# Where the last two projection tiles of a block stand: inside a hand-ordered head, beside sums of squares moved between engines

## The chip, the core and the metric

The kernel runs on one core of a Trainium2 chip. The core has five engines that run their own queues in order and wait for each other through semaphores: TensorE (PE, matmuls; PEld are its weight loads), VectorE (DVE), ScalarE (ACT), GpSimd (POOL) and SyncE (SP, which issues most of the transfers). Matmul results land in PSUM banks; everything else lies in SBUF. The metric is the device time of one execution in microseconds; lower is better. The times are medians of several runs.

## What is computed

A two-layer encoder over two sequences, 256 and 512 tokens, which the kernel keeps side by side as 768 columns. Layer 0 mixes with an mLSTM, layer 1 with windowed attention; each is followed by a gated residual, a modulated norm and a convolutional feed-forward block (FFN):

```python
for l in range(DEPTH):
    mod = jax.nn.silu(c) @ adaln_w[l] + adaln_b[l]
    sh1, sc1, g1, sh2, sc2, g2 = [t[:, None, :] for t in jnp.split(mod, 6, axis=-1)]
    h = rmsnorm(x, norm_g[l, 0]) * (1 + sc1) + sh1
    ...
    y = mlstm_mixer(...) if l % N_MIXERS == 0 else swa_mixer(...)   # both end in "@ w_out"
    x = x + g1 * y
    h = rmsnorm(x, norm_g[l, 1]) * (1 + sc2) + sh2
    x = x + g2 * conv_ffn(h, ffn_w_up[l], ffn_conv_w[l], ffn_conv_b[l], ffn_w_down[l])
return rmsnorm(x, final_g)
```

`rmsnorm` multiplies by `rsqrt(mean(x * x) + EPS)` over the 1024 features. The change touches, in each layer, the end of `@ w_out`, the norm behind it, and the start of `h @ ffn_w_up`.

## The kernel before

**Layout and precision.** Features lie on the 128 partitions, in KC = 8 chunks; tokens run along the free axis. A matrix product in full precision is made of three faster ones: an operand is split into a high part (a rounded copy, made by ScalarE) and a low part (the remainder, a subtraction on VectorE), and high-high, high-low and low-high products are added up in one PSUM bank. `split` (L275) makes `whi` and `wlo` of a weight tile of 128x1024; there are three buffers of each and five of `raw`, into which SP loads.

**The output projection** (`out_proj`, L592) makes 16 tiles: 8 output chunks for the first half of the columns (0 to 383), then 8 for the second half (384 to 767) in the order 5, 6, 7, 4, 0, 1, 2, 3. Below, tile i is the i-th of the 16, from 0. A tile is 24 matmuls of 384 columns (`product`, L632) into one of four fixed banks: tile i takes bank (i + 2) mod 4. Then VectorE adds the gated result to x (`resid`, L590), and ScalarE squares the new x (`Norm.square`, L111). `out_proj` is a generator: the caller runs it as far as its `yield`, then does something else.

**The norm** (`Norm`, L90) has to add up eight squares over chunks and partitions. VectorE adds the squares of the first KC - on_pe chunks into one array (L115; on_pe is 2); TensorE sums the array and the two squares left over the partitions, with a 128x2 constant as the moving operand: 3 arrays x 3 blocks of 128 tokens = 9 matmuls (L146, in the trace `pa<-inv,nt`). ScalarE adds EPS (L150), GpSimd raises to the power -0.5 (L153), and TensorE spreads the result over the partitions (L158, `pa<-kct,nr`). `stages` is a generator whose steps the caller places. `apply` in `combined` (L1095) then scales, shifts and splits the normed values: for the first half at once, for the second half step by step, into combinations called T1, T2, T4, B22 and T3; for T3 it needs the difference of two shifts, `dsh` (L1107).

**The FFN's first product** uses one level of a fast matrix product: B11 and B21 are quarters of the normed values of the first half of the columns, T1 to T4 and B22 belong to the second. `quarters` (L1162) is 12 matmuls of 384 columns for one of them; if `low` is given, it is called after 8 of them. `outset` (L1184) does B11, copies the bank to SBUF (L1189), then adds B21 into the same bank. Sums of weights (`sums`, L1279) are needed as well.

**Who decides the order.** A scheduler orders each engine's instructions by priority and a simulated clock, except in a `manual_schedule` block: there TensorE, ScalarE and VectorE keep the order in which the code is written. `head` (L1257) is such a block; `ffn` runs it for the first pair of hidden tiles, once a layer. Before it, tiles 0 to 14 have been made outside; tile 15 is the first matmul work inside, after two "marks" (L1276, L1277: one matmul each that writes banks 2 and 3, so that later copies into them can be added to). Then come the first quarter, the norm's mean, the second quarter, the spread, and so on; `step()` runs the next part of the norm's generator. `issue_after` (L1420) makes the instructions of the next pair of tiles (`pair`, L1194, whose weight sums run on GpSimd at L1202, L1205, L1206) queue behind named instructions on the same engine.

Of the kernel before, what the change touches and what calls it, by code (L numbers as in the profile page):

```python
# [16 lines left out]
P = 128  # L17
# [67 lines left out]
def pieces(c0, c1):  # L85

    return [(max(c0, s0), min(c1, s1), q) for q, (s0, s1) in enumerate(SEQS) if max(c0, s0) < min(c1, s1)]


class Norm:  # L90
# [16 lines left out]
    def square(self, c):  # L107

        net = self.net
        sq = net.tmp([P, self.n])  # L110
        net.nc.scalar.activation(sq, self.x(c), AF.Square)  # L111
        self.sums.append(sq)
        if 2 <= len(self.sums) and self.count < KC - self.on_pe:
            acc = self.sums[0]
            self.adds.tensor_tensor(acc, acc, self.sums.pop(), ALU.add)  # L115
        self.count += 1

    count = 0

    def begin(self, n):  # L120

        if self.pm is None:
            self.pm = self.net.pa()
            self.sides = [self.pm[:, 2 * b : 2 * b + 2] for b in range(self.n // P)]
            self.done = 0
        for i in range(self.done, n):
            for b, o in enumerate(self.sides):

                self.net.nc.tensor.matmul(
                    o, self.sums[i][:, b * P : (b + 1) * P], self.net.inv,  # L130
                    start=i == b == 0, stop=i == KC - 1, skip_group_check=True,
                )
        self.done = max(self.done, n)

    def stages(self):
# [15 lines left out]
        else:  # L151
            nc.vector.tensor_scalar(r, mean, EPS, None, ALU.add)
        nc.gpsimd.tensor_tensor(r, r, net.mhalf[:, :nb], ALU.pow)  # L153
        yield 2.0
# [13 lines left out]
class Net:  # L168
# [120 lines left out]
    def step(self, gen, n=1):  # L289
        for _ in range(n):  # L290
            next(gen, None)
# [300 lines left out]
    def out_proj(self, u0, act, xt, l, apply):  # L592
# [15 lines left out]

        norms = [Norm(self, xt, half, apply, last=True, adds=self.nc.vector) for half in HALVES]

        self.turn = 1
        todo = tiles()
        if not self.begun:
            first = [next(todo) for _ in range(2)]
            todo = chain(first, todo)
            for i, (z, c, w) in enumerate(first):
                self.product(self.bank[2 + i][:, :H], w, act, 0, H, range(KC - 1))
                self.begun[i] = KC - 1
        for i, (z, c, w) in enumerate(todo):
            if i in (KC, 2 * KC - 1):  # L620
                yield
            c0, c1, _ = HALVES[z]
            o = self.ps()[:, : c1 - c0]
            self.product(o, w, act, c0, c1, range(self.begun.pop(i, 0), KC))
            self.tick(4.2)
            for p0, p1, q in pieces(c0, c1):
                self.resid(xt, o[:, p0 - c0 : p1 - c0], l, 16, c, (p0, p1, q))
            norms[z].square(c)
            if i % KC == KC - 1:
                self.start(HALVES[z], norms[z].stages())  # L630
# [443 lines left out]
    def combined(self, l, i, pool):  # L1074
# [10 lines left out]
        def modulate(b, c, x, pr, rng):  # L1085
            c0, c1, _ = rng
            for p0, p1, q in pieces(c0, c1):
# [5 lines left out]
                nc.scalar.activation(b[:, s], b[:, s], AF.Identity, bias=sh)  # L1093

        def apply(x, pr, rng):  # L1095
            if rng[0] == 0:
                for c in range(KC):
                    full[c] = one(F32)
                    modulate(full[c], c, x, pr, rng)
                    put((self.B11, self.B21)[c // 4], c % 4, full[c])  # L1100
                return
# [4 lines left out]
            sh = lambda c: self.mod[l][:, 24 * i + c, q : q + 1]  # L1106
            dsh = pool.tile([P, 4], F32, name="dsh")  # L1107
            nc.vector.tensor_tensor(
                dsh, self.mod[l][:, 24 * i + 4 : 24 * i + 8, q], self.mod[l][:, 24 * i : 24 * i + 4, q], ALU.subtract
            )  # L1110

# [71 lines left out]

    def outset(self, o, w, r1):  # L1184


        part = lambda i: [t[:, 512 * i : 512 * (i + 1)] for t in w]
        self.quarters(o, part(0), self.B11, True)
        self.nc.scalar.copy(r1[:, col(H) :], o)  # L1189
        yield  # L1190
        self.quarters(o, part(1), self.B21, False)
        self.evict(r1, o)
# [64 lines left out]
    def head(self, u0, last_tile, pool, urows, mark, early):  # L1257
# [21 lines left out]
        def sums(i):  # L1279
            tt = nc.vector.tensor_tensor  # L1280
            s2, s4, s1_, a22 = q[i]
            tt(s1_, s1_, a22, ALU.add)
            nc.scalar.copy(s1[i][0], s1_)
            tt(s2, s1_, s2, ALU.subtract)
            tt(s4, s4, s2, ALU.subtract)
            tt(s1[i][1], s1_, s1[i][0].bitcast(F32), ALU.subtract)
            tt(s1_, a22, s2, ALU.subtract)

        def split(src, to=None):

            hi, lo = to or (self.stg.tile([P, 1024], R, tag=t, name=self.nm(t), bufs=3) for t in ("whi", "wlo"))
            nc.scalar.copy(hi, src)
            return (hi, lo), lambda: nc.vector.tensor_tensor(lo, src, hi.bitcast(F32), ALU.subtract)
# [3 lines left out]
        wa[0] = self.split(ra[0])  # L1297
        sums(0)
        wc[0] = self.split(ra[0])
        for _ in last_tile:  # L1300
            pass
        norm = self.take(HALVES[1])
        step = lambda n=1: [next(norm, None) for _ in range(n)]
        first = self.outset(fixed(0), wa[0], rows[0][0])
        next(first)
        step()
        sums(1)
        wc[1] = self.split(ra[1])
        next(first, None)

        step()
        pa = lambda: self.pa()[:, :H]
# [55 lines left out]
        self.evict(r4, d2)  # L1368
        return act.ins, dve.ins

# [297 lines left out]
```

## Time and profile before

| | |
|---|---|
| median of 3 runs | 1845.19 us (1843.85 to 1846.6) |
| the profiled execution | 1843.78 us |
| its span, first to last instruction | 1842.0 us |
| granted TensorE clock, mean | 0.994 |
| share of the span on the chain that ended last | PE 86%, DVE 6%, DMA 3%, ACT 2%, issue 1%, POOL 1% |

The profile records each instruction of one execution: engine, source line, operation, output and inputs by their names in the program, start and duration. In a timeline row the first two numbers are start and duration in us, `x18` means that 18 instructions were merged into the row, and a bracket gives how long the engine had been idle and what ended it. A row of waits reads "engine, line, waited for engine, line: us in total, times, longest". Matmuls are pipelined, so that their durations overlap; a matmul of 128x384 is followed by the next 0.17 us later. An fp32 matmul of the norm appears as two records. `ps` and `pa` are PSUM banks, `nt` the arrays of squares, `nr` the norm, `slab` large activations. The line is often that of a helper: L254 is any matmul issued through `mm`, L260 and L261 are the two halves of a split.

### The profile page before, as it was taken

The numbers are of one execution on the slowest core, as the hardware profiler recorded it, in microseconds if no ns is written. First come the engines' busy times: TensorE is split into PE (matmuls) and PEld (weight loads), VectorE is DVE, ScalarE is ACT, GpSimd is POOL, SyncE is SP. The second block draws the span as 40 slices with busy tenths as digits, with TensorE's granted clock in tenths as the row PEclk, the third lists the DMA queues.
The fourth block names the chain that finished last, engine by engine and source line by source line (L and its number), as shares of the span: only waits on it lengthen the run. The fifth ranks groups of instructions, "written<-read, shape, count | busy, mean of one in ns | idle before, by whom it ended". The sixth has DMA issues, their size and how long they took to land.

```text
span 1842.0 us, 28931 instructions
## 1 busy us (share of the span) xinstructions
PE 1793.2 (97%) x11290; PEld 1657.4 (90%) x11290; DVE 1367.0 (74%) x2101; ACT 895.3 (49%) x1815; POOL 488.0 (26%) x386
## 2 busy tenths in 40 slices
PE   6999999999999999999999999999999999999997
PEld 3987887889998999999999999889989999999997
DVE  4755676886689877777777757766898777777776
ACT  4443443354456444444444556765564444444443
POOL 1001001021024333333331313430144333333322
PEclk9999999999999999999999999999999999999999
DMA  8344566546312221222223321124122222222212
GB/s 330 119 145 134 172 195 221 164 138 219 101 46 74 76 61 66 69 69 69 69 69 93 104 83 50 53 94 129 50 86 69 69 69 69 69 69 70 69 35 69
DMA packets 64245, 184.48 MB, mean 100 GB/s; under 512 B 6167, under 2 KB 23831, under 8 KB 64108
## 3 DMA queue, kind: packets, MB, share of 16 engines
q1 hardware_dynamic: 64108, 182.63, 30.8%
q8 instruction: 89, 1.46, 0.3%
q14 instruction: 48, 0.39, 0.1%
HBM read 176.17 MB, written 6.43 MB: 99 GB/s over the span
## 4 chain that ended last, share of the span: by engine, by line
PE 86%; DVE 6%; DMA 3%; ACT 2%; issue 1%; POOL 1%; SPq 0%; POOLq 0%; ACTq 0%; DVEq 0%
PE ps L254 27%; PE pa L254 25%; PE ps L1169 10%; PE ps L1172 10%; PE ps L1170 10%; PE pa L1008 1%; DMA slab<-in_adaln_w_dram 1%; DMA raw<-in_w_dram 1%; DVE wlo L261 1%; DVE ada L506 1%; DVE slab L590 1%; DMA raw<-in_adaln_w_dram 0%; PE pa L1172 0%; PE pa L1169 0%; PE pa L1170 0%
## 5 line engine op out<-in xcount | busy, mean ns | idle before, releaser
L260 ACT CAST whi<-raw 128x1024 fp32r<-128x1024 f32 x237 | 247.9, 1048 | 350.4 <-PE pa L254 161.4
L261 DVE TENSOR_TENSOR wlo<-raw,whi 128x1024 fp32r<-128x1024 f32 x237 | 316.6, 1337 | 119.8 <-ACT whi L260 117.3
L254 PE MATMUL pa<-slab,whi 128*128 128x256 f32 (+1 forms) x1472 | 346.6, 331 | 3.2 <-DVE slab L590 3.2
L254 PEld LDWEIGHTS pa<-slab,whi 128*128 128x128 f32 x1472 | 252.7, 188 | 27.5 <-DVE slab L590 4.5
L590 DVE SCALAR_TENSOR_TENSOR slab<-pa,mod,slab 128x256 f32<-128x256 f32 (+1 forms) x368 | 211.2, 592 | 70.8 <-PE pa L254 70.5
L254 PE MATMUL pa<-slab,wlo 128*128 128x256 f32 (+1 forms) x736 | 233.9, 330 | 0.0
L254 PE MATMUL ps<-zh,whi 128*128 128x256 f32 (+1 forms) x560 | 189.0, 339 | 2.3 <-ACT whi L260 1.7
L254 PE MATMUL ps<-zh,wlo 128*128 128x256 f32 (+1 forms) x560 | 184.1, 330 | 2.0 <-DVE wlo L261 2.0
L254 PE MATMUL ps<-zl,whi 128*128 128x256 f32 (+1 forms) x560 | 185.1, 332 | 0.0
L1169 PE MATMUL ps<-zh,whi 128*128 128x384 f32 x504 | 172.3, 342 | 3.6 <-ACT nt L1240 1.8
L1170 PE MATMUL ps<-zl,whi 128*128 128x384 f32 x504 | 169.9, 337 | 0.8 <-DVE zl L1126 0.8
L1172 PE MATMUL ps<-zh,wlo 128*128 128x384 f32 x504 | 168.9, 335 | 0.0
L254 PEld LDWEIGHTS pa<-slab,wlo 128*128 128x128 f32 x736 | 138.5, 188 | 13.1 <-DVE wlo L261 0.4
L1205 POOL TENSOR_TENSOR raw<-raw,raw 128x512 f32<-128x512 f32 x40 | 52.2, 1305 | 330.8 <-DVE wlo L261 259.4
L254 PE MATMUL ps<-slab,whi 128*128 128x384 f32 x512 | 132.0, 339 | 0.9 <-DVE slab L261 0.5
L1402 POOL TENSOR_TENSOR slab<-slab 128x772 f32<-128x772 f32 x44 | 86.5, 1967 | 164.6 <-DVE slab L1390 152.7
L1389 DVE SCALAR_TENSOR_TENSOR slab<-slab,cstt,slab 128x771 f32<-128x771 f32 x88 | 103.6, 1179 | 26.6 <-ACT slab L1387 26.5
L254 PEld LDWEIGHTS ps<-zh,whi 128*128 128x128 f32 x560 | 107.4, 192 | 15.9 <-issue 4.4
L506 DVE SCALAR_TENSOR_TENSOR ada<-raw,silc,ada 128x1024 f32<-128x1024 f32 x84 | 110.6, 1354 | 14.9 <-DMA raw<-in_adaln_w_dram 14.8
L1202 POOL TENSOR_TENSOR raw<-raw 128x512 f32<-128x512 f32 x40 | 68.5, 1712 | 200.1 <-DMA raw<-in_w_dram 169.7
L254 PEld LDWEIGHTS ps<-zh,wlo 128*128 128x128 f32 x560 | 107.2, 192 | 12.2 <-DVE wlo L261 2.9
L254 PEld LDWEIGHTS ps<-zl,whi 128*128 128x128 f32 x560 | 107.4, 192 | 11.9 <-issue 3.4
(291 smaller groups left out, 4265.7 us busy)
## 6 DMA issues: line engine op xcount, KB each, us to landing
raw<-in_w_dram SPq DMA_DIRECT2D x208, 512.0 KB, 3.7
raw<-in_adaln_w_dram SPq DMA_DIRECT2D x84, 512.0 KB, 4.6
slab<-in_x_dram SPq DMA_DIRECT2D x12, 512.0 KB, 6.8
slab<-in_adaln_w_dram SPq DMA_DIRECT2D x12, 512.0 KB, 10.3
slab<-mrows SPq DMA_DIRECT2D x8, 384.0 KB, 5.3
xs<-slab SPq DMA_DIRECT2D x6, 512.0 KB, 3.6
bt<-brow SPq DMA_DIRECT2D x16, 192.0 KB, 3.0
slab<-xs SPq DMA_DIRECT2D x6, 512.0 KB, 6.9
```

What stands on the lines that cost most here:

```text
L254: self.nc.tensor.matmul(out, lhsT, rhs, start=start, stop=stop)
L260: nc.scalar.copy(hi, src)
L261: return nc.vector.tensor_tensor(lo, src, hi.bitcast(F32), ALU.subtract)
L506: stt(acc[:, s], row, w, acc[:, s], ALU.mult, ALU.add)
L590: self.nc.vector.scalar_tensor_tensor(x, o, self.mod[l][:, gc + c, q : q + 1], x, ALU.mult, ALU.add)
L1169: mm(o, wh[:, k], hi[k], start=start and k == 0, stop=False, skip_group_check=True)
L1170: mm(o, wh[:, k], lo[k], start=False, stop=False, skip_group_check=True)
L1172: mm(o, wl[:, k], hi[k], start=False, stop=k == 3, skip_group_check=True)
L1202: tt(q[2], q[2], q[3], ALU.add)
L1205: tt(q[0], q[2], q[0], ALU.subtract)
L1389: stt(y[:, 1:], u[:, :-1], w(0), y[:, 1:], ALU.mult, ALU.add)
L1402: nc.gpsimd.tensor_tensor(y, y, yrow[:, j], ALU.mult)
```

## The change

Half 0 of the norm gets `on_pe` 0 and half 1 gets 1 (`i` of the enumeration): VectorE adds all eight squares of half 0, and seven of half 1. The mean of half 1 is split: `begin(1)` sums the array of seven in the head, ahead of the first quarter, and the last square follows as part of the norm's first step.

`out_proj` yields before tile 14 in place of tile 15, so that tile 14, too, is made inside the head; the weights of tile 15 are drawn (loaded and split) before that yield. Tiles 14 and 15 yield after their product and after their residual and square; their square is added when the head calls `norm.add()`.

In the head, the weight sums of the second pair of tiles and the split behind them go ahead of the first quarter, between the steps of tiles 14 and 15. The norm's first two steps are handed to `outset` as `low`, so they run inside the first and the second quarter. The power's instruction is returned as a third entry of `behind`; as the pair with index 0 takes `behind[0:]` and the one with index 1 `behind[2:]`, GpSimd's work of both next pairs queues behind it. `dsh` is computed at the start of half 0's `apply`.

```diff
@@ Norm
         self.sums.append(sq)
-        if 2 <= len(self.sums) and self.count < KC - self.on_pe:
+        self.count += 1
+        if not self.held:
+            self.add()
+
+    def add(self):
+        if 2 <= len(self.sums) and self.count <= KC - self.on_pe:
             acc = self.sums[0]
             self.adds.tensor_tensor(acc, acc, self.sums.pop(), ALU.add)
-        self.count += 1
+
+    held = False
@@ Norm.begin
-        for i in range(self.done, n):
+        last = min(KC, self.on_pe + 1) - 1
+        for i in range(self.done, min(n, last + 1)):
             for b, o in enumerate(self.sides):
...
-                    start=i == b == 0, stop=i == KC - 1, skip_group_check=True,
+                    start=i == b == 0, stop=i == last, skip_group_check=True,
@@ Norm.stages
-        nc.gpsimd.tensor_tensor(r, r, net.mhalf[:, :nb], ALU.pow)
+        self.power = nc.gpsimd.tensor_tensor(r, r, net.mhalf[:, :nb], ALU.pow)
@@ out_proj
-        norms = [Norm(self, xt, half, apply, last=True, adds=self.nc.vector) for half in HALVES]
+        norms = [Norm(self, xt, half, apply, i, last=True, adds=self.nc.vector) for i, half in enumerate(HALVES)]
+        self.norm = norms[1]
...
-        for i, (z, c, w) in enumerate(todo):
-            if i in (KC, 2 * KC - 1):
+        soon = []
+        for i in range(2 * KC):
+            z, c, w = soon.pop() if soon else next(todo)
+            late = i >= 2 * KC - 2
+            if i == 2 * KC - 2:
+                soon.append(next(todo))
+            if i in (KC, 2 * KC - 2):
                 yield
...
             self.tick(4.2)
+            if late:
+                norms[z].held = True
+                yield
             for p0, p1, q in pieces(c0, c1):
                 self.resid(xt, o[:, p0 - c0 : p1 - c0], l, 16, c, (p0, p1, q))
             norms[z].square(c)
+            if late:
+                yield
@@ combined
+        dsh = pool.tile([P, 4], F32, name="dsh")
+
         def apply(x, pr, rng):
             if rng[0] == 0:
+                s = self.mod[l][:, 24 * i : 24 * i + 8, 0]
+                nc.vector.tensor_tensor(dsh, s[:, 4:], s[:, :4], ALU.subtract)
                 for c in range(KC):
...
-            dsh = pool.tile([P, 4], F32, name="dsh")
-            nc.vector.tensor_tensor(
-                dsh, self.mod[l][:, 24 * i + 4 : 24 * i + 8, q], self.mod[l][:, 24 * i : 24 * i + 4, q], ALU.subtract
-            )
@@ outset
-    def outset(self, o, w, r1):
+    def outset(self, o, w, r1, low=None):
...
-        self.quarters(o, part(0), self.B11, True)
+        self.quarters(o, part(0), self.B11, True, low)
         self.nc.scalar.copy(r1[:, col(H) :], o)
         yield
-        self.quarters(o, part(1), self.B21, False)
+        self.quarters(o, part(1), self.B21, False, low)
@@ head, sums
             tt(s2, s1_, s2, ALU.subtract)
+            yield
             tt(s4, s4, s2, ALU.subtract)
+            yield
             tt(s1[i][1], s1_, s1[i][0].bitcast(F32), ALU.subtract)
             tt(s1_, a22, s2, ALU.subtract)
+            yield
@@ head
         wa[0] = self.split(ra[0])
-        sums(0)
-        wc[0] = self.split(ra[0])
+        ops = [sums(i) for i in range(2)]
+        next(ops[0])
+        next(ops[0])
+        wc[0], low = split(ra[0])
+        next(last_tile)
+        next(last_tile)
+        next(ops[0])
+        low()
+        self.norm.add()
+        next(last_tile)
+        self.norm.begin(1)
+        next(ops[1])
+        next(last_tile)
+        next(ops[1])
+        wc[1], low = split(ra[1])
+        next(ops[1])
+        low()
         for _ in last_tile:
             pass
         norm = self.take(HALVES[1])
         step = lambda n=1: [next(norm, None) for _ in range(n)]
-        first = self.outset(fixed(0), wa[0], rows[0][0])
+        first = self.outset(fixed(0), wa[0], rows[0][0], step)
         next(first)
-        step()
-        sums(1)
-        wc[1] = self.split(ra[1])
         next(first, None)
 
-        step()
...
-        return act.ins, dve.ins
+        return act.ins, dve.ins, self.norm.power.ins
```

## The prediction

> **What bounds the kernel now.** I read the page first, then TensorE's waits over the whole span, then the order of time on each engine around the two heads (layer 0 near 500 us, layer 1 near 1290 us), since the change touches nothing else.
>
> ```profile
> span 1842.0 us, 28931 instructions
> PE 1793.2 (97%) x11290; PEld 1657.4 (90%) x11290; DVE 1367.0 (74%) x2101; ACT 895.3 (49%) x1815; POOL 488.0 (26%) x386
> ```
>
> TensorE (PE) is the bound. An edit pays only if it takes instructions or idle time from PE, and costs only if it puts some in. From the table of PE's waits:
>
> ```profile
> PE ps L1172 <- DVE s1l L261: 2.7, 2, 1.4
> PE pa L254 <- POOL nr L153: 2.5, 4, 1.0
> ...
> PE ps L1169 <- ACT ps L1218: 1.4, 2, 0.7
> ```
>
> Columns: total us, times, longest. Of these only the L153 waits (the power that ends the norm) lie in the stretch that is rewritten. PE there, in order of time (start, duration; a chained matmul starts 0.17 us after the last one, so durations overlap):
>
> ```profile
> 477.63 2.06 PE L254 MATMUL pa<-inv,nt 128*128 128x2 f32 x18
> ...
> 501.36 0.52 PE L254 MATMUL ps<-slab,whi 128*128 128x384 f32 x2
> ...
> 505.57 0.52 PE L254 MATMUL ps<-yh 128*128 128x384 f32 x2
> ...
> 510.12 0.34 PE L1169 MATMUL ps<-yh,whi 128*128 128x384 f32 x1
> ...
> 512.03 0.34 PE L1172 MATMUL ps<-yh,wlo 128*128 128x384 f32 x1
> 512.21 2.06 PE L254 MATMUL pa<-inv,nt 128*128 128x2 f32 x18
> 514.13 0.42 PE L1169 MATMUL ps<-yh,whi 128*128 128x384 f32 x1
> 514.39 0.34 PE L1170 MATMUL ps<-yl,whi 128*128 128x384 f32 x1
> ...
> 516.93 0.93 PE L254 MATMUL pa<-kct,nr 128*128 128x128 f32 x6 [0.47 <-POOL nr L153]
> 517.62 0.42 PE L1169 MATMUL pa<-yh,zh 128*128 128x384 f32 x1
> ```
>
> Half 0's mean stands at 477.63. Tile 14's product starts at 501.36, the two marks at 505.57 with tile 15's product right behind (2 x 0.174 us later, 505.93), the first quarter at 510.12, half 1's mean at 512.21, the second quarter at 514.13; then PE idles 0.47 us for the power before it spreads the norm over the partitions. In layer 1 the same wait is 0.76 us:
>
> ```profile
> 1307.70 0.93 PE L254 MATMUL pa<-kct,nr 128*128 128x128 f32 x6 [0.76 <-POOL nr L153]
> ```
>
> **The change part by part**, per layer, worked in layer 0.
>
> **Squares.** Half 0 now sums all eight squares on VectorE, so its mean takes 3 matmuls in place of 9. The 9 are 18 records; the block is (514.13 - 512.21) / 18 = 0.107 us a record. Twelve records go: **-1.28 us**. Half 1 keeps two sums: 6 matmuls, 12 records, in two blocks. Six records go (-0.64), and one more restart comes: after a block the next matmul follows 0.26 us later (514.13 to 514.39), not 0.17, so +0.09: **-0.55 us**. The Trainium skill, "TensorE: Matmul & The Clock Gate", section "Back-to-back issue gap", gives matmuls of 1 to 64 columns about 25 ns each, or 62 ns where the sequencer decodes them; at 62 ns the 36 records of both layers would be worth 2.2 us in place of 3.85, and the sum below would come out at about -0.1 us. The row speaks against that price here.
>
> The three added VectorE sums per layer cost nothing: half 0's two fall into idle time of the engine, as the first row shows; half 1's is counted in the queue below.
>
> ```profile
> 473.62 0.74 DVE L590 SCALAR_TENSOR_TENSOR slab<-ps,mod,slab 128x128 f32<-128x128 f32 x2 [3.47 <-PE ps L254]
> ...
> 501.56 0.62 DVE L590 SCALAR_TENSOR_TENSOR slab<-ps,mod,slab 128x384 f32<-128x384 f32 x1
> ...
> 502.56 1.22 DVE L261 TENSOR_TENSOR wlo<-raw,whi 128x1024 fp32r<-128x1024 f32 x1
> ...
> 508.06 0.69 DVE L1286 TENSOR_TENSOR s1l<-raw,s1h 128x512 fp32r<-128x512 f32 x1
> 508.78 0.69 DVE L1287 TENSOR_TENSOR raw<-raw,raw 128x512 f32<-128x512 f32 x1
> 509.39 1.22 DVE L261 TENSOR_TENSOR wlo<-raw,whi 128x1024 fp32r<-128x1024 f32 x1
> 510.52 0.61 DVE L590 SCALAR_TENSOR_TENSOR slab<-ps,mod,slab 128x384 f32<-128x384 f32 x1
> 511.05 0.68 DVE L1282 TENSOR_TENSOR raw<-raw 128x512 f32<-128x512 f32 x1
> 511.77 0.69 DVE L1284 TENSOR_TENSOR raw<-raw,raw 128x512 f32<-128x512 f32 x1
> ```
>
> **Tile 14 moves behind the marks.** The marks (L1277) write banks 2 and 3. Tile i lies in bank (i + 2) mod 4, so bank 3 is tile 13's, and it is free only when VectorE has read tile 13's residual: 501.56 + 0.62 = 502.18. Today tile 14's 24 matmuls stand between that product and the marks and hide this. Now tile 14 is in the written order, behind them: the first mark goes at 501.36, the second cannot at 501.53 but only at about 502.23 (0.05 us from the power's end to PE, below). That is 0.70 us idle and 0.09 of restart: **+0.78 us**, a new wait. Behind it stand tiles 14 and 15, thus all of PE. If VectorE is 0.2 us later, so is PE; if nothing has to be waited for, 0. I take 0.78, since the rows fix it. The weights of tile 15 were loaded and split before the head already; their transfer keeps its place in SP's queue (tile 14, tile 15, then four loads of the head), so this edit is worth nothing.
>
> **The norm's steps move into the quarters.** Half 1's first sum goes in a block ahead of the first quarter, the last square and the power after 8 of its 12 matmuls, the spread after 8 of the second quarter's. ScalarE and GpSimd now:
>
> ```profile
> 511.17 0.53 ACT L111 ACTIVATE nt<-slab 128x384 f32<-128x384 f32 x1 [1.86 <-DVE slab L590]
> 512.40 0.48 ACT L1189 COPY slab<-ps 128x384 f32<-128x384 f32 x1 [0.71 <-PE ps L1172]
> 514.31 0.17 ACT L150 ACTIVATE nr<-pa 128x3 f32<-128x3 f32 x1 [1.42 <-PE pa L254]
> ...
> 505.58 1.29 POOL L1202 TENSOR_TENSOR raw<-raw 128x512 f32<-128x512 f32 x1 [24.75 <-DMA raw<-in_w_dram]
> ...
> 514.30 1.30 POOL L1205 TENSOR_TENSOR raw<-raw,raw 128x512 f32<-128x512 f32 x1 [5.94 <-DMA raw<-in_w_dram]
> 515.57 1.31 POOL L153 TENSOR_TENSOR nr<-nr,mhalf 128x3 f32<-128x3 f32 x1
> 516.85 2.31 POOL L1206 TENSOR_TENSOR raw<-raw 128x512 f32<-128x512 f32 x1
> ```
>
> The copy L1189 reads the bank that the second quarter goes on adding to. It runs from 512.40 to 512.88, unseen, because PE is busy with the 18 mean records until 514.13. With the mean inside the quarter nothing stands between the quarters: the second can start 0.37 + 0.48 + 0.05 = 0.90 us after the last matmul of the first (512.03), in place of 0.17. With the restart: **+0.82 us**, a second new wait, with the spread and all later products behind it. Its likes exist: the L1218 waits above, 0.7 us each. Bounds: 0 to about 1.2, if ScalarE is held by the instructions written ahead of the copy (the high half of the fourth weight, about 1.05 us, and L150).
>
> **The power.** It started late behind L1205 of the next pair; now the next pairs' GpSimd work is ordered behind it. Putting 0.78 and the first block (6 x 0.107 + 0.09 = 0.73) in, the first quarter starts at 511.63, the last mean records at 513.02, and L150 runs at about 514.0 (behind that high half). The power, at its present 1.31 us, ends by 515.5. The spread is wanted at 514.45 (quarter's end) + 0.82 + 8 x 0.174 = 516.66. So the wait goes: **-0.47 us, and -0.76 in layer 1**.
>
> **VectorE's written queue.** From tile 14's residual, at product's end 506.71 + 0.20, come L1286, L1287, the low half, the new sum, L1282, L1284, then tile 15's residual. With the spacings of the rows (0.54, 0.72, 0.61, 1.13, 0.47 for the sum, of the size and operation of L1126 with its 0.55, 0.72, 0.61) the sum is done at 510.5, when its block is wanted at 510.90; the residual runs 511.72 to 512.34, the square ends at 512.9, wanted at 513.02. Cost 0, with **0.4 and 0.1 us to spare**; gone, each us costs PE one.
>
> **The shift difference** leaves this place:
>
> ```profile
> 517.93 1.25 DVE L1108 TENSOR_TENSOR dsh<-mod 128x4 f32<-128x4 f32 x1
> 519.10 0.60 DVE L1113 SCALAR_TENSOR_TENSOR slab<-slab,gain,pa 128x384 f32<-128x384 f32 x1
> ...
> 526.13 0.55 DVE L1126 TENSOR_TENSOR zl<-bq,zh 128x384 fp32r<-128x384 f32 x1
> ```
> ```profile
> L530 DVE TENSOR_TENSOR mod<-ps,cstt 128x8 f32<-128x8 f32 x12 | 1.5, 159 | 7.0 <-PE ps L523 7.0
> ```
>
> Its like takes 0.16 us; here it ran under L1206 and took 1.25. Without it, and with the spread earlier, scaling starts at about 517.4 in place of 519.10, while the products behind start 0.5 us later (without half 0's 1.28): VectorE gains some 2.2 us of lead. It had enough: the last low half that T1 needs was done at 526.68, and PE wants T1 at 528.11:
>
> ```profile
> 528.11 0.34 PE L1169 MATMUL ps<-zh,s1h 128*128 128x384 f32 x1
> 529.64 0.56 DVE L1126 TENSOR_TENSOR zl<-bq,zh 128x384 fp32r<-128x384 f32 x1 [0.33 <-ACT zh L1120]
> ```
>
> From there on VectorE waits for ScalarE, whose casts stand in its queue behind copies of PE's products, so the lead ends and the later waits stay: 0. If it did not end, up to 2.2 us a layer (rival 3).
>
> **Sum.** Layer 0: -1.28 - 0.55 - 0.47 + 0.78 + 0.82 = -0.70. Layer 1: -1.28 - 0.55 - 0.76 + 0.78 + 0.82 = -0.99. Together **-1.7 us**. The span goes from 1842.0 to 1840.3 and its execution from 1843.78 to 1842.1; the median of the runs shown, 1845.19, is 1.4 above that execution, so **1843.5 us**.
>
> **The rivals.**
> 1. *A written queue becomes the bound* (slower). VectorE and ScalarE run the head in the order written, with 0.1 us to spare at tile 15's square, and tile 13's residual decides the mark. For it: the little that is spare. Against it: the next pair's GpSimd work no longer runs in this stretch. It decides from 0.85 us of lateness a layer (1.7 / 2). Tile 13's residual behind the first low half and L1282 (1.13 + 0.72 from 502.56 on) comes at 504.4 in place of 501.56: 2.8 us a layer, 5.7 in all, 1843.5 + 5.7 = **1849.2**.
> 2. *The new waits do not open* (faster): the bank or the copy is free when PE gets there. Then only the gains count, -1.28 - 0.55 and the power, -4.9 in all: **1840.3**; with one wait of the two, about 1841.9. For it: PE shows no wait on L1189 now. Against it: both waits follow from rows.
> 3. *The lead carries through* (faster). The wait on s1l, 1.35 us a layer, goes too: -2.7 further, **1840.8**. For it: VectorE is late there, and the lead is larger than the wait. Against it: the cast just shown.
>
> ```profile
> 506.31 1.10 DVE L1284 TENSOR_TENSOR raw<-raw,raw 128x512 f32<-128x512 f32 x1
> ```
>
> 4. *GpSimd's work, pushed behind the power, collides with T1.* L1284 took 1.10 us under L1202 in place of 0.69, the shift difference 1.1 more under L1206. Four such instructions now meet the scaling: 1.6 to 4.4 us of delay against 1.4 + 2.2 of lead; at the worst 0.8 late a layer, **1845.1**. For it: those two; against it: the lead covers all but the worst. The Trainium skill, "SBUF — State Buffer", section "SBUF: two separate sides", says that VectorE with two SBUF inputs and GpSimd hold the shared ports for a whole instruction; by that rule, four blocks of about 1.3 us, 5.2 in all, would leave PE 1.6 us short a layer and the time at 1846.7.
> 5. *The change does not do what it says*: PE's saved records come back as waits for weights. Then 1.2 less of power waits and 3.2 of new waits, **1847.2**. Against it: PE's busy time over 90 us around the head lacks only the 0.47 of the power (columns: stretch, length, busy us and count of each engine, clock, DMA).
>
> ```profile
> 440.00:530.00 90.00, 89.53 (x529) 89.22 (x528) 65.08 (x108) 41.99 (x79) 9.44 (x9) 1.00 0.39 124
> ```
>
> **How the numbers follow.** Forecast 0.36, rival 1 0.20, rival 2 0.22, rival 3 0.15, rivals 4 and 5 together 0.07. Alone the forecast holds 1841.8 to 1845.2 (either wait between 0.4 and 1.2 us). A difference of 0.2%, 3.7 us, is about what a measurement of this kernel can tell from no change. Rivals 2 (with both waits shut) and 3 lie under 1845.2 - 3.7 = 1841.5, so faster has 0.22 + 0.15 = 0.37. Rival 1 lies over 1848.9: slower 0.20. The rest, 0.43, is the same. The range goes from 1839.0, all gains and some of the lead, to 1848.5: what is left out above is rival 1, 2 in 10.
>
> **What would show it.** Half 0's mean as 6 records and half 1's as two blocks of 6; no wait for L153 in the heads; a new wait of about 0.6 us of idle on L590 at the marks, ahead of tile 14; a new wait on L1189 of about 0.6 us ahead of the second quarter; scaling right behind the spread. I am wrong if PE waits for L111 or L115 in the head, if the two new waits are missing, or if the waits after 530 us change.

## The result, and the profile after

| | before | after |
|---|---|---|
| median of 22 runs, us | 1844.79 (1842.79 to 1850.62) | 1841.38 (1839.51 to 1847.91) |
| ratio of the times, 95% interval | 1 | 0.9979 (0.9973 to 0.9985) |
| profiled execution, us | 1843.78 | 1842.62 |

The kernel is 3.4 us faster by the medians, twice the 1.7 us of the forecast. The two profiled executions differ by less, 1.2 us (granted clock 0.994 before, 0.993 after), so what follows compares stretches inside them and leaves the whole time to the medians. From the page after:

```profile
span 1840.5 us, 28864 instructions
PE 1789.9 (97%) x11254; PEld 1652.6 (90%) x11254; DVE 1373.2 (75%) x2107; ACT 896.2 (49%) x1815; POOL 483.8 (26%) x386
```

PE has 36 records less, as planned (12 + 6 in each layer). Its waits over the whole span (total us, times, longest):

```profile
PE ps L1190 <- DVE s1l L268: 2.7, 2, 1.4
...
PE ps L261 <- DVE slab L597: 1.9, 2, 1.0
PE ps L1188 <- DVE zl L1144: 1.8, 5, 0.9
...
PE pa L261 <- POOL nr L160: 1.3, 2, 1.0
PE ps L1187 <- ACT slab L1207: 1.1, 2, 0.6
```

L160, L268, L597 and L1207 are the L153, L261, L590 and L1189 of before. The power's wait (L160) has lost two of its four places, those in the heads. Two new waits stand at the marks (L597) and at the copy (L1207), two times each. The s1l wait has not moved. The wait for low halves (L1144) was 0.8 us in 4 places before; the fifth place is taken up below, with rival 4. PE in layer 0's head, in order of time:

```profile
481.08 0.72 PE L261 MATMUL pa<-inv,nt 128*128 128x2 f32 x6
481.67 0.42 PE L261 MATMUL ps<-slab,wlo 128*128 128x384 f32 x1
...
502.05 0.34 PE L261 MATMUL ps<-yh 128*128 128x384 f32 x1
503.29 0.44 PE L261 MATMUL ps<-yh 128*128 128x384 f32 x1 [0.91 <-DVE slab L597]
503.57 0.51 PE L261 MATMUL ps<-slab,whi 128*128 128x384 f32 x2
...
511.98 0.72 PE L136 MATMUL pa<-inv,nt 128*128 128x2 f32 x6
512.56 0.42 PE L1187 MATMUL ps<-yh,whi 128*128 128x384 f32 x1
...
514.04 0.77 PE L136 MATMUL pa<-inv,nt 128*128 128x2 f32 x6
514.67 0.94 PE L1194 MATMUL ps<-yh,wlo 128*128 128x384 f32 x4
516.18 0.44 PE L1187 MATMUL ps<-yh,whi 128*128 128x384 f32 x1 [0.57 <-ACT slab L1207]
...
517.67 0.83 PE L261 MATMUL pa<-kct,nr 128*128 128x128 f32 x6
518.26 0.94 PE L1194 MATMUL ps<-yh,wlo 128*128 128x384 f32 x4
519.04 0.34 PE L1187 MATMUL pa<-yh,zh 128*128 128x384 f32 x1
...
529.44 0.34 PE L1187 MATMUL ps<-zh,s1h 128*128 128x384 f32 x1
...
1290.51 0.44 PE L261 MATMUL ps<-yh 128*128 128x384 f32 x1 [1.01 <-DVE slab L597]
1316.65 0.34 PE L1187 MATMUL ps<-zh,s1h 128*128 128x384 f32 x1
```

All means are blocks of 6. The second mark waits, the second quarter (516.18) waits, and the spread (517.67) follows its quarter without a wait. The start of the product with T1 (529.44; 528.11 before) can serve as a mark for both kernels. VectorE's residual of tile 7 is another, ahead of everything that the change touches on PE; the rows of after come first, then those of before in layer 1, VectorE's residual and PE's T1:

```profile
475.66 0.74 DVE L597 SCALAR_TENSOR_TENSOR slab<-ps,mod,slab 128x128 f32<-128x128 f32 x2 [2.32 <-PE ps L261]
...
1262.91 0.74 DVE L597 SCALAR_TENSOR_TENSOR slab<-ps,mod,slab 128x128 f32<-128x128 f32 x2 [2.29 <-PE ps L261]
```
```profile
1264.26 0.74 DVE L590 SCALAR_TENSOR_TENSOR slab<-ps,mod,slab 128x128 f32<-128x128 f32 x2 [3.44 <-PE ps L254]
```
```profile
1318.88 0.34 PE L1169 MATMUL ps<-zh,s1h 128*128 128x384 f32 x1
```

From tile 7's residual to T1 it was 528.11 - 473.62 = 54.49 us in layer 0 and 1318.88 - 1264.26 = 54.62 in layer 1; it is 529.44 - 475.66 = 53.78 and 1316.65 - 1262.91 = 53.74. The heads have gained **0.71 and 0.88 us**, 1.6 together, of the 3.4 measured. The rest has to be elsewhere, in code with the same instructions in the same order. The groups of PE's instructions by line, operands and shape (busy us, mean ns of one) show where. Before:

```profile
L1169 PE MATMUL ps<-bq,whi 128*128 128x384 f32 x168 | 57.2, 341 | 0.0
...
L1169 PE MATMUL ps<-zh,s1h 128*128 128x384 f32 x160 | 54.2, 339 | 0.0
```

After:

```profile
L1187 PE MATMUL ps<-bq,whi 128*128 128x384 f32 x168 | 56.5, 336 | 0.0
...
L1187 PE MATMUL ps<-zh,s1h 128*128 128x384 f32 x160 | 53.8, 336 | 0.0
```

Matmuls that read bq or s1h are shorter, in the whole FFN. Such matmuls overlap, so the pace is read better from start to start. The T1 block of 12, from its first row to the first of the next block, took from 528.11 to 530.23 before and from 529.44 to 531.52 after (PE's order of time, before and then after):

```profile
530.23 0.34 PE L1169 MATMUL pa<-yh,zh 128*128 128x384 f32 x1
```
```profile
531.52 0.34 PE L1187 MATMUL pa<-yh,zh 128*128 128x384 f32 x1
```

That is 177 ns a matmul before and 173 after. One thing in the change reaches these tiles without touching an instruction of theirs: `dsh` is now taken from the pool ahead of bq, s1h and s1l, which puts all of them 32 bytes further on in SBUF, as the build lays them out.

### The profile page after: what moved, and what is told of

It reads as the page before. It is cut to its first block, busy times and chain, and to the rows that moved or that the text cites. A ratio compares the mean times of both kernels' runs of the same rounds, so it can differ in the third digit from the quotient of the medians.

```text
span 1840.5 us, 28864 instructions
## 1 busy us (share of the span) xinstructions
PE 1789.9 (97%) x11254; PEld 1652.6 (90%) x11254; DVE 1373.2 (75%) x2107; ACT 896.2 (49%) x1815; POOL 483.8 (26%) x386
## 4 chain that ended last, share of the span: by engine, by line
PE 83%; DVE 6%; issue 4%; ACT 3%; DMA 2%; POOL 1%; SPq 0%; POOLq 0%; ACTq 0%; DVEq 0%
PE pa L261 25%; PE ps L261 25%; PE ps L1187 10%; PE ps L1188 10%; PE ps L1190 10%; PE pa L1026 1%; DMA slab<-in_adaln_w_dram 1%; DVE wlo L268 1%; DVE slab L597 1%; ACT bq L1111 1%; ACT whi L267 1%; DMA raw<-in_adaln_w_dram 0%; PE pa L1190 0%; PE pa L1187 0%; PE pa L1188 0%
## 5 line engine op out<-in xcount | busy, mean ns | idle before, releaser
L267 ACT CAST whi<-raw 128x1024 fp32r<-128x1024 f32 x233 | 243.7, 1048 | 340.1 <-PE pa L261 159.0
L268 DVE TENSOR_TENSOR wlo<-raw,whi 128x1024 fp32r<-128x1024 f32 x233 | 315.9, 1357 | 116.8 <-ACT whi L267 113.0
L261 PE MATMUL pa<-slab,whi 128*128 128x256 f32 (+1 forms) x1472 | 346.6, 331 | 3.2 <-DVE slab L597 3.2
L261 PEld LDWEIGHTS pa<-slab,whi 128*128 128x128 f32 x1472 | 252.6, 188 | 27.6 <-DVE slab L597 4.9
L597 DVE SCALAR_TENSOR_TENSOR slab<-pa,mod,slab 128x256 f32<-128x256 f32 (+1 forms) x368 | 211.4, 593 | 68.6 <-PE pa L261 68.2
L261 PE MATMUL pa<-slab,wlo 128*128 128x256 f32 (+1 forms) x736 | 234.0, 330 | 0.0
L261 PE MATMUL ps<-zh,whi 128*128 128x256 f32 (+1 forms) x560 | 189.0, 338 | 1.8 <-ACT whi L267 1.7
L261 PE MATMUL ps<-zh,wlo 128*128 128x256 f32 (+1 forms) x560 | 184.3, 331 | 2.0 <-DVE wlo L268 2.0
L261 PE MATMUL ps<-zl,whi 128*128 128x256 f32 (+1 forms) x560 | 185.1, 332 | 0.0
L261 PEld LDWEIGHTS pa<-slab,wlo 128*128 128x128 f32 x736 | 138.5, 188 | 13.2 <-DVE wlo L268 0.4
L261 PE MATMUL ps<-slab,whi 128*128 128x384 f32 x512 | 132.3, 339 | 0.9 <-DVE slab L268 0.5
L1421 DVE SCALAR_TENSOR_TENSOR slab<-slab,cstt,slab 128x771 f32<-128x771 f32 x88 | 104.0, 1183 | 26.9 <-ACT slab L1419 26.7
L261 PEld LDWEIGHTS ps<-zh,whi 128*128 128x128 f32 x560 | 107.9, 193 | 15.1 <-issue 4.4
L261 PEld LDWEIGHTS ps<-zh,wlo 128*128 128x128 f32 x560 | 107.6, 192 | 12.0 <-DVE wlo L268 2.9
L261 PEld LDWEIGHTS ps<-zl,whi 128*128 128x128 f32 x560 | 107.7, 193 | 11.8 <-issue 3.4
L1422 DVE SCALAR_TENSOR_TENSOR slab<-slab,cstt,slab 128x771 f32<-128x771 f32 x88 | 110.8, 1259 | 0.8
```

The lines of the kernel that those rows point to most:

```text
L261: self.nc.tensor.matmul(out, lhsT, rhs, start=start, stop=stop)
L268: return nc.vector.tensor_tensor(lo, src, hi.bitcast(F32), ALU.subtract)
L597: self.nc.vector.scalar_tensor_tensor(x, o, self.mod[l][:, gc + c, q : q + 1], x, ALU.mult, ALU.add)
L1421: stt(y[:, 1:], u[:, :-1], w(0), y[:, 1:], ALU.mult, ALU.add)
L1422: stt(y[:, :-1], u[:, 1:], w(2), y[:, :-1], ALU.mult, ALU.add)
```

## The experiments

Two theories stood after the result. **Place:** 1.6 us come from the heads and the rest from the new place of bq and s1 in SBUF. **Heads:** all comes from the heads, and the pace of the FFN differs by chance from one execution to the next. The first four kernels tell them apart; the next four take single steps of the sum; the last three test what was left. In what follows "pace" is the mean time from the start of one matmul to the start of the next, over all of one kind in the trace, with the tenth at each end left out.

### The place alone

```diff
+        dsh = pool.tile([P, 4], F32, name="dsh")
+
         def apply(x, pr, rng):
...
-            dsh = pool.tile([P, 4], F32, name="dsh")
             nc.vector.tensor_tensor(
```

> The kernel before with one line moved: the place of dsh is taken ahead of the bq and s1h/s1l tiles, as in the changed kernel; its subtraction stays where it was, so no instruction moves. In the build this shifts bq and s1h/s1l by 32 bytes in SBUF. Theory (the place of the operands sets the pace): the matmuls that read bq or s1h/s1l go from 176-177 ns to about 173.5 ns from start to start, some 1010 of them, 2.5 to 3.0 us; the time falls by 2.2 to 3.0 us (ratio 0.9984 to 0.9988). Rival (the gain came from the order in the two heads, and the pace differed by chance from execution to execution): ratio 1.0000 within 0.0005, and the pace stays at 176-177 ns.

Measured: 1843.06 us against 1844.88, ratio 0.9992 (0.9983 to 1.0000), 1.8 us less by the medians; the interval just reaches no change. Its groups of PE's instructions:

```profile
L1170 PE MATMUL ps<-bq,whi 128*128 128x384 f32 x168 | 56.5, 336 | 0.0
...
L1170 PE MATMUL ps<-zh,s1h 128*128 128x384 f32 x160 | 53.8, 336 | 0.0
```

The same 336 ns as in the changed kernel, with the instructions and the order of the kernel before. The heads are as long as before (54.53 and 54.56 us from tile 7's residual to T1). The size is somewhat below what was expected, but the direction and the pace are those of the theory. By the paces of the trace the 528 matmuls of bq and the 504 of s1 are 2.9 us shorter together; a new wait ahead of T3 in layer 1, 1.1 us from start to start, takes a part of that back (rival 4, below).

### All tiles of the pool

```diff
+            self.dsh = pool.tile([P, 4], F32, name="dsh")
             self.yh = pool.tile([P, 2, 4, H], R, name="yh")
```

> The kernel before with dsh placed ahead of yh, the first tile of the pool: now yh and yl are shifted by 32 bytes too. Theory: the blocks of yh against weights that are shown at 175 to 176 ns fall to about 173.5 ns as well, some 900 matmuls, another 1.5 to 2.2 us; the time falls by 3.7 to 5 us against the kernel before (ratio 0.9973 to 0.9980). Rival (only bq and s1 are sensitive, through their own neighbours): as the run with dsh ahead of bq, a fall of 2.2 to 3.0 us. Rival (chance): no change.

Measured: 1842.08 us, ratio 0.9985 (0.9977 to 0.9994), 2.8 us less. The yh blocks followed:

```profile
L1169 PE MATMUL ps<-yh,whi 128*128 128x384 f32 x304 | 102.0, 335 | 0.0
```

It was 339 ns before (the row "L1169 PE MATMUL ps<-yh,whi", 103.1 us). The gain is smaller than the 3.7 us expected, and its interval overlaps with that of the run with the place alone, so the pace shows what yh adds better than the time does. It fell short since yl against weights fell only from 175.7 to 174.2 ns, and yh against zh, in the heads, went up from 173.6 to 176.8.

### The order alone

The changed kernel with `dsh` placed behind s1h and s1l, where it was; bq and s1 are taken from the pool first:

```diff
-        dsh = pool.tile([P, 4], F32, name="dsh")
+        late_dsh = []
...
             if rng[0] == 0:
+                full[0] = one(F32)
+                self.s1 = [pool.tile([P, 512], R, tag=t, ...) for t in ("s1h", "s1l")]
+                late_dsh.append(pool.tile([P, 4], F32, name="dsh"))
```

> The changed kernel with every tile of the pool back at the place of the kernel before (dsh is placed behind s1h and s1l again), the order of all instructions as in the changed kernel. Theory: the pace of the bq and s1 blocks is back at 176-177 ns, and what is left is the work on the heads alone: 0.6 us below the kernel before as the two profiles show it, up to 1.7 us as the prediction had it (ratio 0.9991 to 0.9997). Rival (the heads brought the 3.4 us, the place nothing): ratio 0.9979 within 0.0006, as the changed kernel.

Measured: 1844.18 us, ratio 0.9994 (0.9986 to 1.0003), 0.7 us less than before. The interval holds 1.6 us and leaves out the 3.4 of the changed kernel.

Its group of bq against the weights:

```profile
L1192 PE MATMUL ps<-bq,whi 128*128 128x384 f32 x168 | 57.3, 341 | 0.0
```

The pace is that of before, with the order of after. From tile 7's residual to T1 it takes 53.84 and 53.76 us, as in the changed kernel (53.78 and 53.74). The theory of the heads alone falls: the gain is two gains.

### Everything shifted by the same amount

```diff
+        self.dsh = cp.tile([P, 4], F32, name="dsh")
         self.kct = cp.tile([P, 3 * P], F32, name="kct")
```

> The kernel before with dsh placed among the constants, ahead of kct: all tiles behind it, in all pools, shift by 32 bytes, so that the distance between the two operands of nearly every matmul stays as it was. If what counts is that the two operands lie alike modulo 64 bytes, the pace of every block stays (bq and s1 176-177 ns, zh against weights 173.5 ns) and the time is within 0.0005 of the kernel before. If what counts is each operand's own place (32 modulo 64 bytes good, 0 bad), the blocks of zh, slab and the weights lose about 3 ns each and bq and yh win: some 4000 matmuls of 384 columns lose, 8 to 12 us more (ratio 1.004 to 1.007).

Measured: 1845.17 us, ratio 1.0000 (0.9991 to 1.0009). bq against weights stays at 176.1 ns and zh against s1h at 176.8, though each of them lies 32 bytes further on. For a shift of 32 bytes an operand's own place decides nothing; its place against the other operand is what is left.

### One mean alone

```diff
-        norms = [Norm(self, xt, half, apply, last=True, ...) for half in HALVES]
+        norms = [Norm(self, xt, half, apply, n, last=True, ...) for half, n in zip(HALVES, (0, 2))]
```

> The kernel before with one thing of the change alone: half 0's squares are all summed on VectorE, so its mean takes 6 matmuls instead of 18; half 1, the order of the last two tiles and every place in SBUF stay. Theory (12 records less at 0.107 us each, nothing late in their place): 1.28 us less from tile 8's start to tile 14's start in each layer, and 2.6 us less in all (ratio 0.9986). Rival (the two added sums on VectorE make the mean late): the gain in that stretch is under 0.7 us a layer, with a wait on the sum ahead of the mean, and the ratio is above 0.9992.

Measured: 1844.81 us against 1845.11, ratio 0.9993 (0.9983 to 1.0004). Neither theory foresaw what the trace shows. The records are worth what they were priced: from the start of tile 8 to that of tile 14 the kernel takes 1.35 and 1.33 us less, with no wait at the mean. But the wait for the power grew, from 0.47 to 0.83 us in layer 0 and from 0.76 to 1.09 in layer 1. PE, and GpSimd in layer 0:

```profile
515.89 0.93 PE L254 MATMUL pa<-kct,nr 128*128 128x128 f32 x6 [0.83 <-POOL nr L153]
```
```profile
513.27 1.30 POOL L1205 TENSOR_TENSOR raw<-raw,raw 128x512 f32<-128x512 f32 x1 [6.31 <-DMA raw<-in_w_dram]
514.53 1.30 POOL L153 TENSOR_TENSOR nr<-nr,mhalf 128x3 f32<-128x3 f32 x1
```

The power stands behind L1205 of the next pair, and L1205 behind a transfer, so it comes when it comes. About a quarter of the gain runs into it; 1.0 us a layer is left at T1. The interval of the time holds these 2.0 us and no change alike.

### The marks later

```diff
-        for t in banks[0][1:]:
-            mark(t)
...
         next(last_tile)
+        for t in banks[0][1:]:
+            mark(t)
         next(last_tile)
```

> The changed kernel with the two marks issued behind tile 14's product instead of ahead of it. Theory (the wait of 0.91 and 1.01 us at the second mark is new work of the change and lies on the path): the wait is gone, 1.07 and 1.17 us from start to start, 2.2 us less than the changed kernel, which is a ratio of 0.9967 to the kernel before. Rival (tile 15's chain on VectorE and ScalarE gives the lead back): TensorE then waits for tile 15's square or sum ahead of the mean or for the copy or the power longer than now, and the gain over the changed kernel is under 1.0 us.

Measured: 1840.54 us, ratio 0.9972 (0.9963 to 0.9982). The wait at the mark is gone; from tile 7's residual to T1 it takes 526.74 - 473.74 = 53.00 us, 0.78 less than the changed kernel (0.77 in layer 1), not 1.07. Part of the lead comes back at the second block of half 1's mean (VectorE, PE and ScalarE of this run, in order of time):

```profile
473.74 0.74 DVE L597 SCALAR_TENSOR_TENSOR slab<-ps,mod,slab 128x128 f32<-128x128 f32 x2 [2.32 <-PE ps L261]
```
```profile
511.24 0.83 PE L136 MATMUL pa<-inv,nt 128*128 128x2 f32 x6
...
526.74 0.34 PE L1187 MATMUL ps<-zh,s1h 128*128 128x384 f32 x1
```
```profile
510.66 0.53 ACT L111 ACTIVATE nt<-slab 128x384 f32<-128x384 f32 x1 [0.59 <-DVE slab L597]
```

The last square ends at 510.66 + 0.53 = 511.19 and PE goes on at 511.24: the queue that was forecast to have 0.1 us to spare at tile 15's square has none when PE is a microsecond earlier. Over both layers 1.55 us are gained up to T1, between the 2.2 of the theory and the 1.0 of the rival. The time alone does not tell this kernel from the changed one: their intervals overlap.

### A cover for the copy

```diff
         next(first)
-        next(first, None)
...
         second = self.outset(pa(), wa[1], rows[1][0])
         next(second)
         step()
+        next(first, None)
```

> The changed kernel with the first quarter of the second outset put between the two quarters of the first. Theory (the copy of the first quarter is bare): the wait of 0.57 us is gone, 0.81 us from start to start in each layer, 1.6 us less than the changed kernel, which is a ratio of 0.9970 to the kernel before. Rival (the power is next): with it gone TensorE waits for the power ahead of the spread; it ends 0.05 us ahead of the spread's place now and the spread's place comes 0.2 us earlier, so that at most 0.2 us a layer comes back (1.2 us less, ratio 0.9972).

Measured: 1841.54 us, ratio 0.9977 (0.9968 to 0.9986). From tile 7's residual to T1 it takes 0.81 and 0.83 us less than in the changed kernel, with no wait for the copy and none for the power: the price of 0.81 was exact. The time does not show it clearly; 1.6 us lie within the two intervals.

### All three together

The marks later, the cover, and `dsh` ahead of yh.

> The changed kernel with the marks behind tile 14's product, the second outset's first quarter between the first's two, and all tiles of the pool shifted by 32 bytes (dsh ahead of yh). Theory: 2.2 + 1.6 + 1.0 us (the last from the two runs in which the places were shifted, 2.8 less 1.8) below the changed kernel, 8.2 us below the kernel before, a ratio of 0.9956. Rival (one of the two waits comes back in another place): ratio 0.9965 or above.

Measured: **1836.96 us**, ratio 0.9957 (0.9944 to 0.9971), 8.2 us below the kernel before, and by the two intervals faster than the changed kernel too. The heads are 1.64 and 1.57 us shorter up to T1 than those of the changed kernel, 3.2 in all where the theory had 3.8. That the time meets the 8.2 us expected is in part luck.

### The operands between themselves

```diff
         self.zl = self.hp.tile([P, 4, 4, H], R, name="zl")
+        self.dsh = self.hp.tile([P, 4], F32, name="dsh")
```

> The kernel before with dsh placed behind zl: zh and zl stay, all later tiles (weights, slab, yh, bq, s1) shift by 32 bytes. If the pace is set by whether the two operands lie alike modulo 64 bytes: zh against whi/wlo (1536 matmuls of 384 columns, alike before) goes from 173.5 to 176.5 ns, 4.6 us more; zh against s1 (480, unlike before) from 176.5 to 173.5, 1.4 less; bq, yh and slab against the weights keep their distance and their pace; the kernel is some 3 us longer (ratio 1.0017), up to 1.004 if the wider zh blocks lose too. If the rule is another one (zh against weights stays at 173.5 ns), the time is between 1.5 us less and the same.

Measured: 1843.09 us, ratio 0.9990 (0.9981 to 1.0000), 2.0 us less where the expectation left 1.5 at most, and zh against the weights stayed at its pace in the FFN. The rule "alike modulo 64 bytes" is wrong. What holds in these rows is weaker: the pace changes by more than 1.3 ns only where the distance of the two operands does. Pace in ns; bold where the distance differs from before:

| moving, stationary | before | place alone | all of the pool | everything | zl and before fixed |
|---|---|---|---|---|---|
| bq, whi (384 columns) | 176.5 | **173.5** | **173.8** | 176.1 | 175.5 |
| zh, s1h (384) | 176.7 | **173.7** | **173.4** | 176.8 | **173.5** |
| yh, whi (384) | 176.0 | 175.4 | **173.0** | 176.0 | 174.7 |
| yh, zh (384) | 173.6 | 173.8 | **176.8** | 174.3 | **176.2** |
| zh, whi (384, in the FFN) | 174.2 | 174.6 | 174.5 | 174.1 | **174.3** |
| zh, whi (512) | 231.7 | 231.7 | 231.7 | 231.7 | **234.8** |
| whi, zh (256) | 120.0 | 120.0 | 120.0 | 120.0 | **117.1** |

Which distance is the good one for which pair, and why zh against whi does not mind at 384 columns, stays open.

### The shift difference alone

The kernel before with the subtraction ahead of half 0's scaling and every tile at its old place:

```diff
             if rng[0] == 0:
+                s = self.mod[l][:, 24 * i : 24 * i + 8, 0]
+                nc.vector.tensor_tensor(late_dsh[0], s[:, 4:], s[:, :4], ALU.subtract)
...
-            nc.vector.tensor_tensor(
-                dsh, self.mod[l][:, 24 * i + 4 : 24 * i + 8, q], ..., ALU.subtract
```

> The kernel before with the shift difference issued ahead of half 0's scaling, as in the changed kernel, and every tile at its old place in SBUF. Theory (VectorE's lead ends at the casts on ScalarE): scaling of half 1 starts about 1.2 us earlier, the wait for s1l stays at 2.7 us in the whole span, TensorE gains nothing, ratio 1.0000 within 0.0008. Rival (the lead carries through): the s1l wait shrinks and the time falls by up to 2.4 us (ratio 0.9987).

Measured: 1844.58 us against 1845.13, ratio 0.9996 (0.9987 to 1.0005). Of its waits:

```profile
PE ps L1176 <- DVE s1l L261: 2.7, 2, 1.4
```

Counted from tile 7's residual, scaling starts 1.24 us earlier than before. VectorE's lead buys nothing: the s1l wait is what it was, and the time is unchanged within the interval.

### Without the order behind the power

```diff
-        return act.ins, dve.ins, self.norm.power.ins
+        return act.ins, dve.ins
```

> The changed kernel without the order that holds the next pairs' GpSimd work behind the power. Theory (that order is what removed the power's wait): GpSimd's sums of the next pair stand ahead of the power again, the power ends at least one of them (1.3 us) later, and TensorE waits ahead of the spread: the power ends 0.05 to 0.5 us ahead of the spread now, so 0.8 to 1.3 us idle come in each layer, 1.6 to 2.6 us more than the changed kernel (ratio 0.9988 to 0.9995 to the kernel before). Rival (the earlier last square is enough): no wait for the power, ratio 0.9979 within 0.0008.

Measured: 1845.32 us against 1845.13, ratio 1.0005 (0.9996 to 1.0014): the whole gain is gone, 3.6 us by the medians (0.2 above before where the changed kernel is 3.4 below), though bq and s1 keep their new pace. Up to T1 it takes 1.94 and 1.99 us more than the changed kernel. PE and GpSimd in layer 0, then PE in layer 1:

```profile
517.47 0.93 PE L261 MATMUL pa<-kct,nr 128*128 128x128 f32 x6 [1.67 <-POOL nr L160]
```
```profile
512.71 1.68 POOL L1223 TENSOR_TENSOR raw<-raw,raw 128x512 f32<-128x512 f32 x1 [4.54 <-DMA raw<-in_w_dram]
514.47 2.13 POOL L1224 TENSOR_TENSOR raw<-raw 128x512 f32<-128x512 f32 x1
516.56 0.86 POOL L160 TENSOR_TENSOR nr<-nr,mhalf 128x3 f32<-128x3 f32 x1
```
```profile
1308.28 0.94 PE L261 MATMUL pa<-kct,nr 128*128 128x128 f32 x6 [1.68 <-POOL nr L160]
```

Two sums of the next pair, not one, get ahead of the power. The expectation had the mechanism and too small a price.

## Why the prediction was right, and where it was not

The forecast of 1843.5 us (-1.7) was in the right direction at half the size; 1841.38 lies in its range, but below the 1841.8 to which the forecast alone reached, where rivals 2 and 3 stood, and both fall. The sum for the heads, -0.70 and -0.99, came out at -0.71 and -0.88. That it came so near is luck: errors cancelled. For layer 0, from the rows shown:

| term | forecast | measured |
|---|---|---|
| half 0's mean | -1.28 | -1.34: block 481.67 - 481.08 = 0.59, before 479.56 - 477.63 = 1.93 |
| half 1's mean | -0.55 | -0.62: blocks of 0.58 and 0.63 and one restart of 0.09 more, before 514.13 - 512.21 = 1.92 |
| power's wait | -0.47 | -0.74: see below |
| marks' wait | +0.78 | +1.16: 503.57 - 502.05 = 1.52, without a wait 505.93 - 505.57 = 0.36 |
| copy's wait | +0.82 | +0.82: 516.18 - (514.67 + 0.09 + 4 x 0.174) = 0.72, and 0.1 of restart |

The five together make -0.72. The end of half 0's mean before, in PE's order of time:

```profile
479.56 0.60 PE L254 MATMUL ps<-slab,whi 128*128 128x384 f32 x2
```

**The step that failed** is the one on the shift difference, with its result "0". It priced the instruction that was moved, and rightly, as the run with that instruction alone shows. But the step also moved where `dsh` is stored, and with it bq and s1. That is worth 1.8 us by the medians of the run with the place alone, and it is the half of the gain that was missing. No term and no rival held it.

**The power** was mis-sized. The forecast took the idle time of the row. An idle time counts from the end of the last matmul, 0.34 us after its start, while chained starts follow after 0.17, and a restart costs another 0.1. From the last matmul's start to the spread it took 516.93 - 516.12 = 0.81 us before and takes 517.67 - 517.50 = 0.17 now; the spread itself took 517.62 - 516.93 = 0.69 and takes 518.26 - 517.67 = 0.59. Together that is 0.74. The two new waits had been priced in this way; the one removed had not. The two quarters' last matmuls ahead of the spread, before and after:

```profile
516.12 0.34 PE L1172 MATMUL ps<-yh,wlo 128*128 128x384 f32 x1
```
```profile
517.50 0.34 PE L1188 MATMUL ps<-yl,whi 128*128 128x384 f32 x1
```

**The marks** cost 0.4 us more. The forecast read tile 13's residual off rows of the kernel before, where it starts 501.56 - 501.36 = 0.20 us after PE has gone on to tile 14. Now it starts 502.63 - 502.05 = 0.58 us after PE has gone on to the first mark. It stands directly behind the low half of tile 15's weights on VectorE, as it did before (first row: before; then after):

```profile
500.34 1.21 DVE L261 TENSOR_TENSOR wlo<-raw,whi 128x1024 fp32r<-128x1024 f32 x1
```
```profile
501.49 1.22 DVE L268 TENSOR_TENSOR wlo<-raw,whi 128x1024 fp32r<-128x1024 f32 x1
502.63 0.61 DVE L597 SCALAR_TENSOR_TENSOR slab<-ps,mod,slab 128x384 f32<-128x384 f32 x1
```

So the place of tile 15's split, put at nothing, is not what cost it. In the run with one mean alone, where tiles and marks stand as before, the residual also starts 500.54 - 499.96 = 0.58 us after tile 14 (PE, then VectorE):

```profile
499.96 0.52 PE L254 MATMUL ps<-slab,whi 128*128 128x384 f32 x2
```
```profile
500.54 0.61 DVE L590 SCALAR_TENSOR_TENSOR slab<-ps,mod,slab 128x384 f32<-128x384 f32 x1
```

The shorter mean of half 0 alone thus moves the residual against PE: from tile 7's residual on, tile 14 comes 1.35 us earlier in that run and tile 13's residual 0.97. Layer 1 shows the same: 0.20 us before, 0.66 in that run, 0.68 in the changed kernel. The forecast's first term changed the rows from which it read its marks. Why VectorE follows only in part was not tested.

**VectorE's queue** for tile 15 held as forecast, with 0.1 us to spare: no wait in the heads is for L111 or L120. With the marks out of the way it does bind, by 0.3 us.

**The rivals.** Rival 1 named the right place, tile 13's residual behind other work, at a seventh of its price. Rival 2 falls: both waits opened. Rival 3 falls, by the s1l wait and by the run with the shift difference alone. Rival 4 shows nothing in PE up to T1. Later, in layer 1 alone, there is one more wait, 0.94 us for a low half of T3: VectorE's last two took 2.28 us with a GpSimd sum beside them, 1.22 before. By the forecast's own signs, waits that change after 530 us speak against it. But the pushed work is not what brings it. The run with the place alone, in the old order, has one of 0.97 at the same place, and so have the runs with all of the pool shifted and with the cover; the changed order with the old places has none. It shows only where bq and s1 are shifted, though not in every such run. The total of the run with the place alone:

```profile
PE ps L1171 <- DVE zl L1127: 1.8, 5, 1.0
```

Rival 5 falls: the saved records stayed saved. The rule of 62 ns a small matmul from the Trainium skill, "TensorE: Matmul & The Clock Gate", section "Back-to-back issue gap", would have made half 0's 12 records worth 0.74 us; the trace has 1.34, or 0.11 us a record.

## What to carry to other kernels

A line that moves an allocation is a change of its own: list which buffers it shifts and compare the pace of the matmuls that read them, also far from the edited code. Price every wait, removed or new, from start to start of what stands around it, never from the idle column alone, and ask of each row that a price is read from whether another edit of the same change moves it. And where work of one engine is ordered behind a short step that TensorE waits for, try the kernel without that order: here its absence cost as much as the whole change gained.

## What the runs showed of the hardware

A shift of one operand by 32 bytes in SBUF can change the pace of matmuls of 384 columns by some 3 ns in 176, in either direction (zh against whi did not mind), and the same shift of both operands changed it by less than 1 ns. By the medians it is worth 1.8 us of 1845 in the run with the place alone, and another 1.0 where yh was shifted too (the first interval just reaches no change, and the intervals of the two runs overlap). It is a matter of whole blocks: yh against zh lost in the very kernel in which yh against whi won. What in the memory or the engine does this no run shows.
